# Modulation blocks of the two mixers on ScalarE and GpSimd instead of TensorE

## The chip, the cores and the metric

The kernel runs on one core of a Trainium2 chip. The time is that of one execution in device microseconds (us); of several runs the median counts. The engines are TensorE (PE in the profile, PEld for its weight loads), VectorE (DVE), ScalarE (ACT), GpSimd (POOL) and SyncE (SP), which issues the loads.

## The reference

Two layers of an encoder over 256 tokens of width 1024. In each layer a vector `c` of 1024 numbers gives six modulation vectors of 1024, which shift, scale and gate the layer's two parts: a mixer (a recurrence beside attention) and a feed-forward part, which is dense in layer 0 and a choice of 2 of 8 experts in layer 1.

```python
c_act = jax.nn.silu(c)
for l in range(DEPTH):
    mod = c_act @ ada_w[l] + ada_b[l]                 # 1024 x 6144 per layer
    shift1, scale1, gate1, shift2, scale2, gate2 = [m[:, None, :] for m in jnp.split(mod, 6, axis=-1)]
    h = rms_norm(x, norm1_g[l]) * (1 + scale1) + shift1
    ...                                               # input projection, recurrence, attention
    x = x + gate1 * ((g_lru * y_lru + g_mla * y_mla) @ w_out[l])
    h = rms_norm(x, norm2_g[l]) * (1 + scale2) + shift2
    ...                                               # feed-forward part f
    x = x + gate2 * f
```

The product `c_act @ ada_w[l]` is what the change is about. It is a row vector times a matrix of 24 MB per layer.

## The kernel before, in words

**Weights.** Every weight matrix is streamed once, in tiles of 1 MB (four times 128 rows by 512 columns of float32). SyncE issues the loads into a ring of four tiles, `raw0` to `raw3` (`load`, L148); a tile's slot is free again once its last reader is done. Where a matrix goes through TensorE in full precision, `split` (L176, L177) makes two halves of it: ACT casts the upper one (`wh`), DVE subtracts it for the lower one (`wl`), and each product is three matmuls (`mm3`, L309 to L311). So ACT and DVE work on every tile, and PE waits for both.

**Modulation.** The 6144 columns of a layer are cut into blocks of 512, called (layer, group, block); groups 0 to 5 are shift1, scale1, gate1, shift2, scale2, gate2. A block is two tiles of 1 MB, the halves of its 1024 rows. Most blocks are computed beside the dense part or ahead of the first mixer, by DVE (`ada`, L394, and others). Eight are computed inside the mixers by `ada_pe`: in mixer 0 the blocks 2_0, 2_1 (gate1), 4_0, 4_1 (scale2), 3_0, 3_1 (shift2) of layer 0; in mixer 1 the blocks 5_0, 5_1 (gate2) of layer 1. There PE multiplies each 128x512 piece by `c32`, a column of `c_act` widened to 32 columns, into a quarter of one PSUM tile (L363, eight matmuls per block). The tile is copied to `aacc` in SBUF: with the bias row added by DVE (L369) in the row blocks, groups 2 and 5, or by ACT (L371) in the column blocks, groups 3 and 4.

**What follows a block.** `ada_done` lets GpSimd sum `aacc` over the 128 partitions (`partition_all_reduce`, L318, a routine from a library). For a row block that is the end: the result is the gate row. For a column block GpSimd then keeps a diagonal (`affine_select`, L321), and `ada_cols` lets ACT sum it into columns (four activations, L341, the first ordered behind the cast that was last issued), to which DVE adds the bias (L348). `ada_cols` runs when a later block takes its accumulator, and once more at the mixer's end.

**The mixer.** `mixer` writes the work as a sequence of weight tiles: latents, `ck`, `q`, `kv`, then 16 tiles `t0` to `t15`, then the output projections. Its table `adas` says behind which tile a block stands. Eight attention heads (`head`, L976) and the steps of the recurrence hang on units of the same sequence. Attention normalizes q and k: GpSimd adds the epsilon and raises to the power -1/2 (`head_norm`, L938 and L939, into `rk` and `rq`); DVE scales the row maxima by `rq` (L997) and ACT the exponentials (L1000). GpSimd has little else to do.

**Order.** Each engine runs its own instructions in their order, and waits for others by semaphores. That order is made when the program is built, by a scheduler that goes by its own estimates of durations; `pr.order` adds a rule that one instruction stands behind another. So moving a block moves many instructions around it.

Of the kernel before, what the change touches and what calls it, by code (L numbers as in the profile page):

```python
# [14 lines left out]
AF = mybir.ActivationFunctionType  # L15
OP = mybir.AluOpType
# [4 lines left out]
D = 1024  # L21
# [200 lines left out]
def encoder(ctx: ExitStack, tc, x, c, positions, params, ada_w, ada_b, w_in, w_uq, w_ukv, w_o_mla,  # L222
            lru_gate_w, w_o_lru, w_out, ffn_w_gate, ffn_w_up, ffn_w_down, moe_router,
            moe_w_gate, moe_w_up, moe_w_down, out):
    nc = tc.nc
    V, A, G, T = nc.vector, nc.scalar, nc.gpsimd, nc.tensor
# [33 lines left out]
    cact = ct("cact", [P, KD])  # L260
    c32 = ct("c32", [P, KD, 32])
# [20 lines left out]
    brow = bt("brow", [P, 512])  # L282
# [5 lines left out]
    pr = Program(tc, list(cut_ring), dma_ahead=3, split_ahead=2)  # L288
# [11 lines left out]
    cur = {}  # L300
# [27 lines left out]
    def ada_acc(nm, more):  # L328
        n_acc[0] += 1
        if ada_q and ada_q[0][4] <= n_acc[0] - (ADA_KEEP if more else 1):  # L330
            ada_cols()
        tag, b = (("lraw0", 1), ("aacc", 2), ("lraw1", 1), ("aacc", 2))[n_acc[0] % 4] if more else ("aacc", 2)
        return wp.tile([P, 512], F32, tag=tag, name=f"aacc_{nm}", bufs=b)
# [16 lines left out]
            rn = (R_N1 if grp == 1 else R_N2) + 4 * blk  # L350
            V.scalar_tensor_tensor(dst, dst, 1.0, cols[l][:, rn:rn + 4], op0=OP.add, op1=OP.mult)

    def ada_pe(l, grp, blk, ring="a"):

        nm = f"{l}_{grp}_{blk}"
        box = {}

        def half(h, raw):
            if h == 0:
                box["ps"] = cur["ada_ps"](f"apa_{nm}")  # L360
            ps = box["ps"]
            for kk in range(4):
                T.matmul(ps[32 * kk:32 * kk + 32, :], c32[:, 4 * h + kk, :], raw[:, kk, :], start=h == 0, stop=h == 1)  # L363
            if h == 0:
                return
            acc = ada_acc(nm, False)
            if grp in (2, 5):
                nc.sync.dma_start(brow[0:1, :], ada_b[l:l + 1, grp * D + 512 * blk:grp * D + 512 * blk + 512])
                V.tensor_add(acc, ps, brow)  # L369
            else:  # L370
                A.copy(acc, ps)  # L371
            ada_done(l, grp, blk, acc)

        for h in range(2):
            W(ada_w[l], 4 * h, 4, grp * D + 512 * blk, 512, "raw", lambda raw, h=h: half(h, raw), ring)
# [223 lines left out]
    def mixer(l):  # L599
# [525 lines left out]
        def half_tiles(ap, c0, acc_fn, i):  # L1125
            W(ap, 4 * i, 4, c0, 512, "k", lambda q, h_, l_: acc_fn(4 * i + 2 * q, h_, l_))

        adas = {0: {"ck": (0, 2, 0), "q": (0, 2, 1), "t5": (0, 4, 0), "t7": (0, 4, 1), "t9": (0, 3, 0), "t11": (0, 3, 1)},
                1: {"t7": (1, 5, 0), "t9": (1, 5, 1)}}[l]

        def mark(name):
            if name in adas:
                ada_pe(*adas[name])

        def chunks(pos):
            for k in range(KD):
# [791 lines left out]
```

## Time and profile before

| | |
|---|---|
| median of 3 runs | 1452.67 us (1451.45 to 1455.13) |
| the profiled execution | 1453.3 us, span 1451.6 us |
| PE busy | 1390.5 us, 96% of the span |
| DVE busy | 1061.6 us, 73% |
| ACT busy | 840.8 us, 58% |
| GpSimd busy | 144.3 us, 10% |

The span is what the profiler saw from the first instruction to the last of one execution; the rest of the execution's time lies around it. A busy share is an average over the whole program; the work of the change stands in two stretches, mixer 0 (to about 263 us) and mixer 1 (about 560 to 660 us). Rows of a timeline give the start and the duration in us, and in brackets how long the engine sat idle before and what it waited for ("issue": for nothing that the profile shows).

### The profile page before, as it was taken

The numbers are of one execution on the slowest core, as the hardware profiler recorded it, in microseconds if no ns is written. First come the engines' busy times: TensorE is split into PE (matmuls) and PEld (weight loads), VectorE is DVE, ScalarE is ACT, GpSimd is POOL, SyncE is SP. The second block draws the span as 40 slices with busy tenths as digits, with TensorE's granted clock in tenths as the row PEclk, the third lists the DMA queues.
The fourth block names the chain that finished last, engine by engine and source line by source line (L and its number), as shares of the span: only waits on it lengthen the run. The fifth ranks groups of instructions, "written<-read, shape, count | busy, mean of one in ns | idle before, by whom it ended". The sixth has DMA issues, their size and how long they took to land.

```text
span 1451.6 us, 20969 instructions
## 1 busy us (share of the span) xinstructions
PE 1390.5 (96%) x7786; PEld 1058.7 (73%) x7786; DVE 1061.6 (73%) x1460; ACT 840.8 (58%) x1279; POOL 144.3 (10%) x116
## 2 busy tenths in 40 slices
PE   7999999899999899999999999999999999999997
PEld 5977667799988788677877744788784368888732
DVE  4799877799899499877599613898882069988711
ACT  3678854544544498854388513787781167877500
POOL 1021220033232002010021000000000000000000
PEclk8999999999999999999999999999999999999999
DMA  9784667989986254565778999999899999998996
GB/s 320 248 261 131 232 235 240 306 291 320 320 307 220 87 175 158 173 208 204 291 280 312 335 409 414 411 388 397 279 388 378 403 408 400 378 360 312 384 399 268
DMA packets 169134, 436.59 MB, mean 301 GB/s; under 512 B 7336, under 2 KB 63016, under 8 KB 157760
## 3 DMA queue, kind: packets, MB, share of 16 engines
q1 hardware_dynamic: 168400, 434.48, 81.8%
q8 instruction: 63, 1.03, 0.3%
q10 hardware_dynamic: 560, 0.66, 0.1%
q14 instruction: 47, 0.39, 0.1%
q0 software_dynamic: 64, 0.03, 0.0%
HBM read 434.10 MB, written 1.05 MB: 300 GB/s over the span
## 4 chain that ended last, share of the span: by engine, by line
PE 71%; DVE 16%; issue 5%; ACT 4%; DMA 2%; POOL 1%; SPq 0%; DVEq 0%; ACTq 0%; POOLq 0%
DVE wl L177 7%; PE eg L1752 4%; PE dn L310 4%; PE dn L1775 4%; PE dn L311 4%; PE eu L1752 4%; PE dn L309 4%; PE eg L310 3%; PE eg L311 3%; PE eg L309 3%; PE eu L310 3%; PE eu L309 3%; PE eu L311 3%; DVE aacc L394 2%; PE u L309 1%
## 5 line engine op out<-in xcount | busy, mean ns | idle before, releaser
L177 DVE TENSOR_TENSOR wl<-wr,wh 128x1024 fp32r<-128x1024 f32 (+2 forms) x556 | 638.9, 1182 | 86.2 <-ACT wh L176 83.1
L176 ACT CAST wh<-wr 128x1024 fp32r<-128x1024 f32 (+2 forms) x556 | 547.1, 1000 | 207.1 <-PE dn L311 31.7
L1673 DVE TENSOR_TENSOR act<-sg,eu 128x512 f32<-128x512 f32 (+2 forms) x42 | 25.1, 612 | 143.6 <-PE eu L1752 102.5
L310 PE MATMUL eg<-wl,xe 128*128 128x512 f32 x240 | 91.7, 382 | 4.2 <-DVE wl L177 2.9
L310 PE MATMUL eu<-wl,xe 128*128 128x512 f32 x240 | 90.4, 377 | 1.6 <-DVE wl L177 1.6
L311 PE MATMUL eu<-wh,xe 128*128 128x512 f32 x240 | 89.8, 374 | 0.0
L311 PE MATMUL eg<-wh,xe 128*128 128x512 f32 x240 | 89.7, 374 | 0.0
L310 PE MATMUL dn<-wl,ahl 128*128 128x512 f32 x220 | 87.5, 401 | 0.8 <-DVE wl L177 0.8
L311 PE MATMUL dn<-wh,ahl 128*128 128x512 f32 x220 | 85.8, 393 | 0.0
L309 PE MATMUL eg<-wh,xe 128*128 128x512 f32 x240 | 81.0, 379 | 0.0
L309 PE MATMUL eu<-wh,xe 128*128 128x512 f32 x240 | 80.4, 374 | 0.0
L394 DVE SCALAR_TENSOR_TENSOR aacc<-wr,cact,aacc 128x512 f32<-128x512 f32 x84 | 74.9, 895 | 1.1
L309 PE MATMUL dn<-wh,ahl 128*128 128x512 f32 x220 | 75.7, 397 | 0.0
L1752 PE MATMUL eu<-wr,xe 128*64 128x512 f32 (+1 forms) x288 | 66.0, 562 | 0.0
L1752 PE MATMUL eg<-wr,xe 128*64 128x512 f32 (+1 forms) x288 | 65.3, 564 | 0.0
L1664 ACT ACTIVATE sg<-eg 128x512 f32<-128x512 f32 (+2 forms) x42 | 20.6, 534 | 73.2 <-PE eg L1752 73.2
L318 POOL PARTITION_ALL_REDUCE aacc<-aacc x12 | 49.0, 4083 | 132.7 <-DVE aacc L394 67.9
L1775 PE MATMUL dn<-wr,aT 128*64 128x512 f32 x264 | 58.9, 596 | 0.0
L310 PEld LDWEIGHTS eg<-wl,xe 128*128 128x128 f32 x240 | 45.2, 188 | 16.0 <-DVE wl L177 7.2
L310 PE MATMUL g<-wl,hTh 128*128 128x512 f32 x128 | 51.8, 405 | 2.8 <-DVE wl L177 2.8
L310 PEld LDWEIGHTS eu<-wl,xe 128*128 128x128 f32 x240 | 45.1, 188 | 12.3 <-DVE wl L177 3.3
L309 PE MATMUL g<-wh,hTh 128*128 128x512 f32 x128 | 52.8, 418 | 0.0
(422 smaller groups left out, 3205.1 us busy)
## 6 DMA issues: line engine op xcount, KB each, us to landing
wr<-in_moe_w_down_dram SPq DMA_DIRECT2D x88, 1024.0 KB, 7.8
wr<-in_moe_w_gate_dram SPq DMA_DIRECT2D x64, 1024.0 KB, 9.4
wr<-in_moe_w_up_dram SPq DMA_DIRECT2D x64, 1024.0 KB, 7.7
wr<-in_ada_w_dram SPq DMA_DIRECT2D x48, 1024.0 KB, 7.7
wr<-in_w_in_dram SPq DMA_DIRECT2D x30, 1024.0 KB, 5.3
wr<-in_moe_w_gate_dram SPq DMA_DIRECT2D x32, 768.0 KB, 11.0
wr<-in_moe_w_up_dram SPq DMA_DIRECT2D x32, 768.0 KB, 5.7
wr<-in_ffn_w_gate_dram SPq DMA_DIRECT2D x13, 1024.0 KB, 8.0
```

Of the source, the lines that this page charges most:

```text
L176: i1 = self.nc.scalar.copy(hi, src)
L177: i2 = self.nc.vector.tensor_sub(lo, src, hi.bitcast(F32))
L309: T.matmul(o, lh, rh, start=start, stop=False)
L310: T.matmul(o, lh, rl, start=False, stop=False)
L311: T.matmul(o, ll, rh, start=False, stop=stop)
L318: G.partition_all_reduce(tot, acc, P, bass_isa.ReduceOp.add)
L394: V.scalar_tensor_tensor(acc, raw[:, kk, :], cact[:, k:k + 1], acc, op0=OP.mult, op1=OP.add)
L1664: A.activation(sg[r, cs_], p[r, cs_], AF.Silu)
L1673: V.tensor_mul(act[r, cs_], B["sg"][j][r, cs_], p[r, cs_])
L1752: T.matmul(ps[0][64 * j:64 * j + 64, :sl.stop - sl.start], B["xe", e][:, k, :], raw[:, sl], start=k == 0, stop=k == KD - 1)
L1775: T.matmul(B["dn"][0][64 * m:64 * m + 64, :], a_, raw[:, 512 * m:512 * m + 512], start=f == 0, stop=f == FC - 1)
```

## The change

The eight blocks are computed by `ada_mix` in place of `ada_pe`. Of the four 128x512 pieces of a tile, two are multiplied by their entry of `c_act` in place by ACT, two by GpSimd (both L363 in the changed file); GpSimd adds the pieces, and in row blocks the bias row, into `aacc` (L372, L374, L377). The PSUM tile and its copy are gone; `ada_done` and `ada_cols` are unchanged. The first of ACT's products of each half stands behind the cast that was last issued. Five of the six blocks of mixer 0 and one of mixer 1 stand behind another tile than before. In all 64 matmuls, four DVE adds and four ACT copies go, and 32 ACT products, 32 GpSimd products and 60 GpSimd additions come. Lines behind the new function lie 7 further down (L938 becomes L945, L997 becomes L1004, L1000 becomes L1007).

```diff
--- before.py
+++ after.py
@@ -350,26 +350,33 @@
             rn = (R_N1 if grp == 1 else R_N2) + 4 * blk
             V.scalar_tensor_tensor(dst, dst, 1.0, cols[l][:, rn:rn + 4], op0=OP.add, op1=OP.mult)
 
-    def ada_pe(l, grp, blk, ring="a"):
+    def ada_mix(l, grp, blk, ring="a"):
 
         nm = f"{l}_{grp}_{blk}"
+        rowk = grp in (2, 5)
         box = {}
 
         def half(h, raw):
+            for kk in range(4):
+                k = 4 * h + kk
+                if kk % 2:
+                    G.tensor_scalar(raw[:, kk, :], raw[:, kk, :], cact[:, k:k + 1], None, op0=OP.mult)
+                    continue
+                i1 = A.activation(raw[:, kk, :], raw[:, kk, :], AF.Copy, scale=cact[:, k:k + 1])
+                if kk == 0:
+                    pr.order(i1, pr.last[0])
             if h == 0:
-                box["ps"] = cur["ada_ps"](f"apa_{nm}")
-            ps = box["ps"]
-            for kk in range(4):
-                T.matmul(ps[32 * kk:32 * kk + 32, :], c32[:, 4 * h + kk, :], raw[:, kk, :], start=h == 0, stop=h == 1)
-            if h == 0:
-                return
-            acc = ada_acc(nm, False)
-            if grp in (2, 5):
-                nc.sync.dma_start(brow[0:1, :], ada_b[l:l + 1, grp * D + 512 * blk:grp * D + 512 * blk + 512])
-                V.tensor_add(acc, ps, brow)
-            else:
-                A.copy(acc, ps)
-            ada_done(l, grp, blk, acc)
+                acc = box["acc"] = ada_acc(nm, False)
+                if rowk:
+                    nc.sync.dma_start(brow[0:1, :], ada_b[l:l + 1, grp * D + 512 * blk:grp * D + 512 * blk + 512])
+                    G.tensor_tensor(acc, raw[:, 0, :], brow, op=OP.add)
+                else:
+                    G.tensor_tensor(acc, raw[:, 0, :], raw[:, 1, :], op=OP.add)
+            acc = box["acc"]
+            for kk in range(0 if h else 1 if rowk else 2, 4):
+                G.tensor_tensor(acc, acc, raw[:, kk, :], op=OP.add)
+            if h:
+                ada_done(l, grp, blk, acc)
 
         for h in range(2):
             W(ada_w[l], 4 * h, 4, grp * D + 512 * blk, 512, "raw", lambda raw, h=h: half(h, raw), ring)
@@ -1125,12 +1132,12 @@
         def half_tiles(ap, c0, acc_fn, i):
             W(ap, 4 * i, 4, c0, 512, "k", lambda q, h_, l_: acc_fn(4 * i + 2 * q, h_, l_))
 
-        adas = {0: {"ck": (0, 2, 0), "q": (0, 2, 1), "t5": (0, 4, 0), "t7": (0, 4, 1), "t9": (0, 3, 0), "t11": (0, 3, 1)},
-                1: {"t7": (1, 5, 0), "t9": (1, 5, 1)}}[l]
+        adas = {0: {"ck": (0, 2, 0), "t1": (0, 2, 1), "t4": (0, 4, 0), "t6": (0, 4, 1), "t8": (0, 3, 0), "t10": (0, 3, 1)},
+                1: {"t7": (1, 5, 0), "t10": (1, 5, 1)}}[l]
 
         def mark(name):
             if name in adas:
-                ada_pe(*adas[name])
+                ada_mix(*adas[name])
 
         def chunks(pos):
             for k in range(KD):
```

The scheduler's order of GpSimd's instructions shows a row that the source does not name: a bare `ISA`, ahead of a library routine that follows arithmetic and ahead of arithmetic that follows a library routine. In the trace of the kernel before it is called MODIFY_POOL_CONFIG. The first place is GpSimd's queue in mixer 0 from the end of block 2_0 to the normalizations of k and q (`vv`, `rk`, `rq`); before:

```order
L318 ISA gate_103<-aacc_2_0_861 128x512
L952 COPY k_869<-kr_645 128x8x32 x2
L318 ISA gate_103<-aacc_2_1_928 128x512
L938 ISA
L938 TENSOR_SCALAR vv_1190<-vv_1190 128x16
L939 TENSOR_TENSOR rk_1189<-vv_1190,mhalf 128x16
L938 TENSOR_SCALAR vv_1307<-vv_1307 128x16
L939 TENSOR_TENSOR rq_1306<-vv_1307,mhalf 128x16
```

After, from the normalization of k on (`wr` are the tiles of ada_w, `cact` is silu of c):

```order
L945 TENSOR_SCALAR vv_1179<-vv_1179 128x16
L372 TENSOR_TENSOR aacc_2_1_1257<-wr_1040,brow 128x512
L946 TENSOR_TENSOR rk_1178<-vv_1179,mhalf 128x16
L377 TENSOR_TENSOR aacc_2_1_1257<-aacc_2_1_1257,wr_1040 128x512 x3
L377 TENSOR_TENSOR aacc_2_1_1257<-aacc_2_1_1257,wr_1071 128x512 x4
L318 ISA
L318 ISA gate_103<-aacc_2_1_1257 128x512
L945 ISA
L945 TENSOR_SCALAR vv_1319<-vv_1319 128x16
L363 TENSOR_SCALAR wr_1276<-wr_1276,cact 128x512
L946 TENSOR_TENSOR rq_1318<-vv_1319,mhalf 128x16
```

The whole of block 2_1 and two bare ISA rows now stand between the two normalizations.

The second place is GpSimd's queue for the column blocks 4_1 and 3_0 of mixer 0; before:

```order
L318 ISA aacc_4_1_1883<-aacc_4_1_1883 128x512
L321 AFFINE_SELECT aacc_4_1_1883<-aacc_4_1_1883 128x512
L318 ISA aacc_3_0_2014<-aacc_3_0_2014 128x512
L321 AFFINE_SELECT aacc_3_0_2014<-aacc_3_0_2014 128x512
```

After, from the reduction of 4_1 to that of 3_0:

```order
L318 ISA aacc_4_1_1822<-aacc_4_1_1822 128x512
L374 ISA
L374 TENSOR_TENSOR aacc_3_0_1959<-wr_1774 128x512
L321 AFFINE_SELECT aacc_4_1_1822<-aacc_4_1_1822 128x512
L377 TENSOR_TENSOR aacc_3_0_1959<-aacc_3_0_1959,wr_1774 128x512
L363 TENSOR_SCALAR wr_1806<-wr_1806,cact 128x512
L377 TENSOR_TENSOR aacc_3_0_1959<-aacc_3_0_1959,wr_1774 128x512
L363 TENSOR_SCALAR wr_1806<-wr_1806,cact 128x512
L377 TENSOR_TENSOR aacc_3_0_1959<-aacc_3_0_1959,wr_1806 128x512 x4
L318 ISA
L318 ISA aacc_3_0_1959<-aacc_3_0_1959 128x512
```

Between two reductions there are now nine or more instructions of arithmetic and two bare ISA rows, where there was one selection. In all, the bare rows go from 3 to 11 in mixer 0 and from 1 to 3 in mixer 1.

The third place is ACT's queue around its reading of block 3_1, the last of mixer 0 (L341); before, up to the second head behind it:

```order
L371 COPY aacc_3_1_2171<-apa_3_1_0_2153 128x512
L341 ACTIVATE aacc_3_1_2171,ada_100<-aacc_3_1_2171 128x128 x3
L176 CAST wh_2195<-wr_2111 128x1024
...
L1000 ACTIVATE pr_0_2264,sm_0_2261<-s_0_2257,mx_0_2260,rq_1306 128x256 x2
...
L341 ACTIVATE aacc_3_1_2171,ada_100<-aacc_3_1_2171 128x128
L1000 ACTIVATE pr_0_2349,sm_0_2346<-s_0_2342,mx_0_2345,rq_1306 128x256 x2
```

After:

```order
L1007 ACTIVATE pr_0_2296,sm_0_2293<-s_0_2289,mx_0_2292,rq_1318 128x256 x2
...
L1007 ACTIVATE pr_0_2381,sm_0_2378<-s_0_2374,mx_0_2377,rq_1318 128x256 x2
L176 CAST wh_2245<-wr_2132 128x1024
L176 CAST wh_2261<-wr_2132 128x1024
L341 ACTIVATE aacc_3_1_2147,ada_100<-aacc_3_1_2147 128x128 x3
L176 CAST wh_2313<-wr_2165 128x1024
L176 CAST wh_2331<-wr_2165 128x1024
```

The last two heads (L1007) stand ahead of the reading of block 3_1 where they stood behind it, and the casts of the output projections follow it.

## Rows read from the trace of the kernel before

**Rows 1.** The page, parts 1 and 4: busy time by engine; the chain by engine.
```profile
PE 1390.5 (96%) x7786; PEld 1058.7 (73%) x7786; DVE 1061.6 (73%) x1460; ACT 840.8 (58%) x1279; POOL 144.3 (10%) x116
...
PE 71%; DVE 16%; issue 5%; ACT 4%; DMA 2%; POOL 1%; SPq 0%; DVEq 0%; ACTq 0%; POOLq 0%
```

**Rows 2.** Windows: stretch, length, busy us (instructions) of PE, PEld, DVE, ACT, POOL; clock, DMA.
```profile
60.00:140.00 80.00, 73.91 (x492) 62.52 (x491) 74.63 (x134) 64.55 (x117) 17.22 (x10) 1.00 0.65 211
140.00:220.00 80.00, 76.72 (x381) 54.41 (x382) 62.32 (x106) 55.37 (x121) 19.03 (x8) 0.98 0.65 224
560.00:640.00 80.00, 75.11 (x399) 56.90 (x400) 74.77 (x135) 60.22 (x103) 11.53 (x4) 1.00 0.53 178
```

**Rows 3.** Windows, L363 alone: stretch, length, busy us of PE and PEld.
```profile
60.00:260.00 200.00, 13.62 (x96) 2.75 (x96) 0.99 0.67 224
560.00:660.00 100.00, 3.85 (x32) 0.84 (x32) 1.00 0.52 174
```

**Rows 4.** Groups of POOL's instructions by form: busy us, mean ns; idle before.
```profile
L318 POOL PARTITION_ALL_REDUCE aacc<-aacc x12 | 49.0, 4083 | 132.7 <-DVE aacc L394 67.9 <-ACT aacc L371 64.8
L318 POOL PARTITION_ALL_REDUCE gate<-aacc x8 | 30.3, 3787 | 128.4 <-DVE aacc L394 61.9 <-DVE aacc L369 59.6 <-issue 6.9
L321 POOL TENSOR_SCALAR_AFFINE_SELECT aacc<-aacc 128x512 f32<-128x512 f32 x12 | 13.8, 1148 | 0.9
L1538 POOL TENSOR_TENSOR xr<-xr,xn 128x512 f32<-128x512 f32 x4 | 6.8, 1691 | 34.5 <-ACT xn L1533 34.5
...
L1540 POOL TENSOR_TENSOR xn<-xr,xn 128x512 bf16<-128x512 f32 x4 | 5.6, 1388 | 12.3 <-ACT xn L1536 12.3
```

**Rows 5.** Timeline of POOL in mixer 0: start us, duration us, instruction, idle before.
```profile
71.51 1.25 POOL L908 TENSOR_TENSOR rs<-ssq,mhalf 128x4 f32<-128x4 f32 x1
79.67 3.25 POOL L318 PARTITION_ALL_REDUCE gate<-aacc  x1 [6.90 <-issue]
...
107.26 1.09 POOL L938 TENSOR_SCALAR vv<-vv 128x16 f32<-128x16 f32 x1 [15.90 <-DVE vv L937]
...
122.29 3.20 POOL L939 TENSOR_TENSOR rq<-vv,mhalf 128x16 f32<-128x16 f32 x1
155.53 3.25 POOL L318 PARTITION_ALL_REDUCE aacc<-aacc  x1 [30.05 <-ACT aacc L371]
...
205.62 3.31 POOL L318 PARTITION_ALL_REDUCE aacc<-aacc  x1 [14.57 <-ACT aacc L371]
209.01 0.63 POOL L321 TENSOR_SCALAR_AFFINE_SELECT aacc<-aacc 128x512 f32<-128x512 f32 x1
```

**Rows 6.** Timeline around 75 us, DVE.
```profile
75.33 0.69 DVE L369 TENSOR_TENSOR aacc<-apa,brow 128x512 f32<-128x512 f32 x1
```

**Rows 7.** Groups of ACT's instructions by form.
```profile
L176 ACT CAST wh<-wr 128x512 fp32r<-128x512 f32 x16 | 10.0, 623 | 0.4 <-PE y L310 0.4
```

**Rows 8.** Timeline in the expert part, 747 to 756 us, DVE and POOL.
```profile
747.09 1.22 DVE L177 TENSOR_TENSOR wl<-wr,wh 128x1024 fp32r<-128x1024 f32 x1
747.15 2.18 POOL L1538 TENSOR_TENSOR xr<-xr,xn 128x512 f32<-128x512 f32 x1 [2.06 <-ACT xn L1533]
...
748.33 2.08 DVE L177 TENSOR_TENSOR wl<-wr,wh 128x1024 fp32r<-128x1024 f32 x1
...
755.23 1.17 POOL L1540 TENSOR_TENSOR xn<-xr,xn 128x512 bf16<-128x512 f32 x1 [5.90 <-ACT xn L1536]
```

**Rows 9.** Line L318: durations in ns (least, median, most), first and last start.
```profile
L318 POOLq MODIFY_POOL_CONFIG  x8: 6/8/11, 72.7 to 570.4; - x8
```

**Rows 10.** Timeline from 470 to 481 us, the end of the dense part, ACT and POOL.
```profile
472.44 0.19 ACT L427 ACTIVATION_READ_ACCUMULATOR fax<-xs 128x1 f32 x1
...
479.75 0.30 POOL L451 TENSOR_SCALAR nrv<-ss 128x1 f32<-128x1 f32 x1 [7.52 <-issue]
```

**Rows 11.** DMA issues from 100 to 210 us: count, size, median us to landing.
```profile
wr<-in_ada_w_dram SPq DMA_DIRECT2D x8, 1024.0 KB, 5.3
```

**Rows 12.** Timeline around 136 us, DVE.
```profile
135.86 0.16 DVE L997 TENSOR_TENSOR mx<-mx,rq 128x2 f32<-128x2 f32 x1
```

**Rows 13.** Timeline of ACT from 200 to 263 us.
```profile
209.68 0.31 ACT L341 ACTIVATE aacc<-aacc 128x128 f32<-128x128 f32 x1 [4.15 <-POOL aacc L321]
...
262.70 1.06 ACT L176 CAST wh<-wr 128x1024 fp32r<-128x1024 f32 x1 [1.62 <-PE wo L311]
```

## The prediction

> **What bounds the kernel now.** I read the page's first and fourth parts first: TensorE (PE) is busy 96% of the span and makes 71% of the chain that ended last, while GpSimd (POOL) is busy 10%, 116 instructions in all [rows 1]. That says where the weight of the whole lies, not what the two mixers can bear. So the next view was the busy time of each engine in the stretches where the blocks stand: mixer 0 from 60 to 220 us and mixer 1 from 560 to 640 us [rows 2]. PE has 74 to 77 of each 80 us, and VectorE (DVE) nearly as much: 5.4, 17.7 and 5.2 us idle in the three. ScalarE (ACT) has 15 to 25 us idle, and GpSimd 61 to 68. What is removed from PE comes from the same view of L363 alone [rows 3]: 13.62 us in mixer 0 and 3.85 us in mixer 1, 17.5 in all. GpSimd's own rows, by group and one by one, then price what is added [rows 4, 5].
>
> **The change part by part.**
>
> *Removed.* 17.5 us of PE, of which the share on the chain would be a gain if everything else stayed covered. Also four DVE adds at 0.69 [rows 6], 2.7 us, and four ACT copies of the same size.
>
> *Products on ACT.* 32 copies with a scale, priced by the cast of a 128x512 tile at 0.623 [rows 7]: 15 us in mixer 0 against 40 idle [rows 2]. I cost them at nothing themselves; their place matters below.
>
> *GpSimd's arithmetic.* A row block has 4 products and 8 additions on GpSimd, a column block 4 and 7. For an addition the rows give a mean of 1.691 and 1.388 and single ones of 1.17 and 2.18 [rows 4, 8]; I take 1.4, near the cheaper group since the dear one has more contention in it, with ends of 1.17 and 2.18. A product reads one tensor; the nearest row is the affine selection over 128x512, 0.63 at its shortest and 1.148 in the mean [rows 4, 5]: 0.8, ends 0.63 and 1.15.
>
> *GpSimd's library switch.* This is the term that the diff does not show. In the order, a bare ISA row stands wherever GpSimd goes from tensor arithmetic to the partition reduction, or back; in the trace the same thing is a MODIFY_POOL_CONFIG [rows 9]. Its price: after the power at 71.51 (1.25 us) GpSimd has nothing to run until the reduction at 79.67, 6.90 us of "issue", though that reduction's input came from DVE at 75.33 + 0.69 = 76.0 [rows 5, 6]. On the way back, the mean square was read out at 472.44 + 0.19 = 472.6, and the first arithmetic row starts at 479.75, behind 7.52 us of "issue" [rows 10]. So about 7.2 us in either direction. Before, almost every switch lies in a pause: the reductions at 155.53 to 205.62 stand 13 to 21 us apart with no arithmetic between them [rows 5]. After, mixer 0 has 11 such rows instead of 3, and mixer 1 has 3 instead of 1.
>
> The Trainium skill, GPSIMD Engine Reference, section 2.1, says that the first call after new code is loaded pays some 6 us, measured 5.95. This trace has 6.90 and 7.52, and the measurement decides; by the page's figure the nine switches below would cost 11 us less.
>
> *The chain on GpSimd in mixer 0.* Per column block: 4 x 0.8 + 7 x 1.4 + reduction 4.1 + selection 1.15 + two switches 14.4 = 32.6 us, against 13 to 21 between reductions before. So GpSimd sets the pace. I sum it from the normalization of k, whose input comes at 107.26 [rows 5], later by 2.7 because DVE has been held back by the first block: 110. Behind it on GpSimd, in the changed order, stand 36 additions (50.4), 16 products (12.8), 9 switches (64.8), 5 reductions at 4 (20), 4 selections (4.6), and the two normalizations at 0.8 + 3.2 (8.0): 160.6 us. To this come waits, which I put at 13.8: 5 for ACT's products of block 2_1, queued behind activations of the recurrence, and 8.8 for tiles whose slot comes free late and whose 1 MB takes 5.3 us to land [rows 11]. End of block 3_1: 110 + 160.6 + 13.8 = 284.4, where before it was 209.01 + 0.63 = 209.7.
>
> Two things hang on this chain. The power for q, ready at 125.5 before [rows 5], comes behind block 2_1 and both its switches: 110 + 4 + 11.2 + 5 + 7.2 + 4 + 7.2 + 0.8 + 0.8 + 3.2 = 153. Its first reader on DVE stood at 135.86 [rows 12], so DVE waits some 15 us there with the lower halves of the weights queued behind it, and PE with DVE. And ACT's reading of block 3_1, which waited 4.15 us before [rows 13], has the mixer's remaining casts queued behind it. Before, 262.7 - 209.7 = 53.0 us passed from there to the mixer's last cast [rows 13]; in the changed order two heads stand ahead of it, and I take 11 us off that rest. Mixer 0: 284.4 - 209.7 - 11 = +64.
>
> The ends: with 1.17 and 0.63 and no waits the chain ends at 259.6, +39; with 2.18 and 1.15 at 318, +98.
>
> *Mixer 1.* Two row blocks put 28.8 us of arithmetic, 8 of reductions and 21.6 of switches on GpSimd, where 11.53 of 80 us are used [rows 2]. It just fits. What remains is a tile or two loaded late, since a block holds its two slots until its last addition, and DVE's losses (next paragraph): +5, between -3.85 (all hidden, PE's share gone) and +16 (DVE's whole loss, no idle time used).
>
> *The port.* With GpSimd adding from 747.15 to 749.33, DVE's subtraction at 748.33 took 2.08 us, where the one before took 1.22 [rows 8]. So an addition on GpSimd takes about 0.8 from DVE; a product, with half the operands, I estimate at 0.4. In mixer 0 that is 44 x 0.8 + 24 x 0.4 = 45 us against 23 idle. In the forecast these losses lie mostly inside the stretches in which DVE waits for GpSimd, so they aren't added.
>
> The Trainium skill, SBUF — State Buffer, "SBUF: two separate sides", calls the shared ports an exclusive lock: the engine that comes second waits for the whole instruction. The trace agrees, 2.08 beside 1.22 [rows 8]; by that rule alone, without switches, the time is that of rival A.
>
> *Sum.* +64 + 5 = +69 on the profiled execution's 1453.3 us: 1522.3. The median of the runs lies 0.6 under that execution, so 1521.
>
> **Rivals.**
>
> A, the port alone: the switches overlap other work, and only DVE's losses tell. Mixer 0: 45 - 23 idle - 2.7 for the removed adds = 19; mixer 1: 16 - 5.2 idle = 11. 1483. For it: DVE is 93% busy in two of the stretches [rows 2]. Against it: 6.90 and 7.52 us in which GpSimd ran nothing [rows 5, 10], and additions that leave it no pause.
>
> B, PE's gain: GpSimd's long chain is covered, because nobody needs the modulation before the mixer's end, and PE's 17.5 us count with its 71% of the chain: -12.4, 1440. For it: 61 to 68 us idle on GpSimd in each stretch [rows 2]. Against it: the powers for k and q are in GpSimd's queue, and ACT waited on block 3_1 already before [rows 13]. It decides once a column block costs less than its spacing, 13 to 21 us; I work out 32.6.
>
> C, one direction of the switch costs nothing, because the arithmetic never leaves memory: 4 switches fewer on the chain, 284.4 - 28.8, so +35 + 5: 1493. Against it: 7.52 on the way back [rows 10].
>
> D, every GpSimd operation at its contended price: 1453.3 + 98 + 11 = 1562. For it: DVE leaves few pauses in which GpSimd can take the port. Against it: DVE itself stalls as soon as GpSimd sets the pace, and that frees the port.
>
> **How the numbers follow.** The forecast 0.66, A 0.14, C 0.08, D 0.06, B 0.06. A measurement of this kernel tells a change from none from about 0.3%, 4.4 us. Faster is B, 0.06. The same is the edge of A in which DVE's pauses take all of the losses, 0.03. Slower is the rest, 0.91. The range takes in A and C, and the forecast's ends (1453.3 + 39 - 3.85 - 0.6 = 1488 below, 1453.3 + 98 + 16 - 0.6 = 1567 above) except its dearest part: 1470 to 1550. Left out are B, D, the edge of A and some 0.04 of the forecast's own top, 0.19 together.
>
> **What would show it.** Right: gaps of about 7 us marked "issue" before the reductions and before the first arithmetic after them; ACT's reading of block 3_1 (L341) idle for tens of us on GpSimd's L321; DVE idle for some 15 us on the power for q; GpSimd busy far beyond 144 us, and PE idle between 200 and 300 us. The port: the mean of L177 above 1182 ns. Wrong: a reduction that starts as soon as its additions end, or a mixer 0 whose last cast still stands near 263 us. If L177 grows but no engine waits long on GpSimd, it was A; if PE's idle time in mixer 0 shrinks, B.

## The result and the profile after

The changed kernel takes 1550.38 us in the median (1549.09 to 1551.35, 4 runs) against 1453.08 us before: a ratio of 1.067 (95% interval 1.0655 to 1.0682). It is slower, as forecast, by 97 us where 69 were forecast; the median lies just above the top of the range.

The page of the kernel after, parts 1 and 4, to be held against [rows 1]:

```profile
PE 1405.4 (91%) x7658; PEld 1076.6 (69%) x7658; DVE 1095.5 (71%) x1456; ACT 859.3 (55%) x1307; POOL 292.7 (19%) x208
...
PE 57%; DVE 16%; issue 9%; POOL 9%; DMA 4%; ACT 4%; SPq 1%; DVEq 0%; POOLq 0%; ACTq 0%
```

GpSimd is still busy only 19% of the span. It has 9% of the last chain, though, where it had 1%. "Issue", the kind of wait under which the library switches show, went from 5% to 9%, and PE's share fell from 71% to 57%.

Where the time went is read from three marks that both kernels pass: GpSimd's first row of the norm behind mixer 0 (L451 before, L458 after), the same behind the dense part, and the reduction of the router's bias at mixer 1's end. In the kernel after:

```profile
346.18 0.62 POOL L458 TENSOR_SCALAR nrv<-ss 128x1 f32<-128x1 f32 x1 [12.31 <-ACT ax L434]
...
560.01 0.31 POOL L458 TENSOR_SCALAR nrv<-ss 128x1 f32<-128x1 f32 x1 [7.08 <-issue]
...
773.84 1.31 POOL L1068 PARTITION_ALL_REDUCE rbias<-rbias  x1
```

Before, the second stood at 479.75 [rows 10], the first and the third here:

```profile
269.20 0.62 POOL L451 TENSOR_SCALAR nrv<-ss 128x1 f32<-128x1 f32 x1 [11.80 <-ACT ax L427]
...
676.05 1.37 POOL L1061 PARTITION_ALL_REDUCE rbias<-rbias  x1
```

So mixer 0 lost 77.0 us, the dense part 3.3 and mixer 1 17.5; from there to the end both kernels take 775.6 to 775.9 us.

The stretches of mixer 0 after, in the columns of [rows 2]:

```profile
60.00:140.00 80.00, 62.02 (x371) 58.02 (x370) 74.76 (x105) 56.74 (x104) 50.27 (x30) 0.81 0.55 175
140.00:220.00 80.00, 57.03 (x255) 41.97 (x254) 52.85 (x84) 49.21 (x93) 46.25 (x29) 0.87 0.32 107
220.00:300.00 80.00, 51.53 (x181) 37.24 (x181) 42.72 (x63) 28.46 (x61) 41.41 (x26) 0.76 0.46 155
```

No engine is near full after 140 us. That is how a chain of waits looks: PE falls to 51.5 of 80 us and the loads to 107 GB/s, where they had 224. The mean of the granted clock, 1.00 and 0.98 before [rows 2], is 0.76 to 0.87, so for a part of these stretches TensorE ran at the lower of its two levels. GpSimd has much of that chain. Its timeline for the last column block (3_1), with the switches on both sides:

```profile
261.34 3.25 POOL L318 PARTITION_ALL_REDUCE aacc<-aacc  x1 [8.02 <-issue]
271.76 1.57 POOL L363 TENSOR_SCALAR wr<-wr,cact 128x512 f32<-128x512 f32 x1 [7.17 <-issue]
273.31 0.64 POOL L321 TENSOR_SCALAR_AFFINE_SELECT aacc<-aacc 128x512 f32<-128x512 f32 x1
273.95 1.55 POOL L363 TENSOR_SCALAR wr<-wr,cact 128x512 f32<-128x512 f32 x1
275.48 1.25 POOL L374 TENSOR_TENSOR aacc<-wr 128x512 f32<-128x512 f32 x1
276.73 1.55 POOL L363 TENSOR_SCALAR wr<-wr,cact 128x512 f32<-128x512 f32 x1
278.26 1.25 POOL L377 TENSOR_TENSOR aacc<-aacc,wr 128x512 f32<-128x512 f32 x1
279.50 1.60 POOL L363 TENSOR_SCALAR wr<-wr,cact 128x512 f32<-128x512 f32 x1
281.06 6.62 POOL L377 TENSOR_TENSOR aacc<-aacc,wr 128x512 f32<-128x512 f32 x5
295.57 3.74 POOL L318 PARTITION_ALL_REDUCE aacc<-aacc  x1 [7.88 <-issue]
```

From one reduction to the next pass 34.2 us without another wait: two switches of 7.17 and 7.88, and arithmetic end to end between them. Before, the spacing was 13 to 21 us [rows 5]. One thing was not forecast: a product (L363) takes 1.55 to 1.60 us even where an addition takes 1.25.

### The profile page after: what moved, and what is told of

Its sections match the earlier page's. It is cut to its first block, busy times and chain, and to the rows that moved or that the text cites. A ratio compares the mean times of both kernels' runs of the same rounds, so it can differ in the third digit from the quotient of the medians.

```text
span 1549.7 us, 20872 instructions
## 1 busy us (share of the span) xinstructions
PE 1405.4 (91%) x7658; PEld 1076.6 (69%) x7658; DVE 1095.5 (71%) x1456; ACT 859.3 (55%) x1307; POOL 292.7 (19%) x208
## 4 chain that ended last, share of the span: by engine, by line
PE 57%; DVE 16%; issue 9%; POOL 9%; DMA 4%; ACT 4%; SPq 1%; DVEq 0%; POOLq 0%; ACTq 0%
DVE wl L177 7%; PE eg L1759 4%; PE dn L1782 4%; PE eu L1759 4%; PE dn L310 3%; PE dn L311 3%; PE dn L309 3%; POOL aacc L377 3%; DVE aacc L401 3%; PE eg L310 3%; PE eg L311 3%; PE eg L309 3%; POOL wr L363 3%; PE eu L310 2%; PE eu L309 2%
## 5 line engine op out<-in xcount | busy, mean ns | idle before, releaser
L177 DVE TENSOR_TENSOR wl<-wr,wh 128x1024 fp32r<-128x1024 f32 (+2 forms) x556 | 649.9, 1204 | 116.0 <-ACT wh L176 112.7
L363 POOL TENSOR_SCALAR wr<-wr,cact 128x512 f32<-128x512 f32 x32 | 68.2, 2134 | 94.7 <-DMA wr<-in_ada_w_dram 51.1
L377 POOL TENSOR_TENSOR aacc<-aacc,wr 128x512 f32<-128x512 f32 x52 | 76.0, 1461 | 3.0
L310 PE MATMUL g<-wl,hTh 128*128 128x512 f32 x128 | 56.5, 441 | 18.5 <-DVE wl L177 18.4
L318 POOL PARTITION_ALL_REDUCE aacc<-aacc x12 | 44.7, 3721 | 99.1 <-DVE aacc L401 66.6
```

Source lines behind the costliest of these rows:

```text
L177: i2 = self.nc.vector.tensor_sub(lo, src, hi.bitcast(F32))
L310: T.matmul(o, lh, rl, start=False, stop=False)
L318: G.partition_all_reduce(tot, acc, P, bass_isa.ReduceOp.add)
L363: G.tensor_scalar(raw[:, kk, :], raw[:, kk, :], cact[:, k:k + 1], None, op0=OP.mult)
L377: G.tensor_tensor(acc, acc, raw[:, kk, :], op=OP.add)
```

## The experiments

Marks as above; "m0" is what mixer 0 lost against the profiled execution before (269.2 us), "m1" the length of mixer 1 (196.3 before).

| kernel | median us | m0 | m1 |
|---|---|---|---|
| changed | 1550.4 | +77.0 | 213.8 |
| TensorE sums over the partitions | 1528.5 | +54.4 | 221.0 |
| GpSimd on 8 of 512 columns | 1494.0 | +31.6 | 200.8 |
| all products on ACT | 1534.4 | +70.0 | 207.3 |
| places of before | 1574.8 | +94.5 | 218.7 |
| TensorE's sum one block later | 1510.1 | +43.9 | 211.7 |
| before, with GpSimd copies | 1496.8 | +30.1 | 207.0 |
| without ACT's rule | 1555.2 | +79.3 | 215.3 |
| before, with TensorE's sum | 1460.9 | +6.8 | 202.1 |
| late sum, tiles released early | 1501.6 | +38.8 | 212.3 |
| late sum, 8 of 512 columns | 1458.2 | -1.4 | 205.2 |
| products in other forms | 1550.0 | +75.3 | 213.8 |
| before, at the new places | 1465.5 | +20.2 | 195.3 |
| two more switches per block | 1631.4 | +148.3 | 226.7 |
| mixer 0 only | 1539.4 | +78.9 | 196.4 |

The kernel before ran at 1453.2 to 1454.8 beside them (medians). Where the profiled execution is not the median, m0 and the median differ by some us (the profiled one took 1474.3 us for "before, at the new places" and 1639.1 for "two more switches").

In five kernels TensorE sums in both mixers: runs 1, 5, 8, 9 and 10 below. There the last mark, itself a library routine, is the first one behind arithmetic, and it stands behind a gap of its own of 5.8 to 6.0 us. From that mark to the end these kernels take 769.7 to 770.3 us, where the others take 775.6 to 777.6. So their m1 is to be read some 6 us shorter: mixer 1 of run 1, for one, is about as long as that of the change, and that of run 8 as long as before.

**1. No library routine in the mixers.**

```diff
-                ada_done(l, grp, blk, acc)
+                ada_red(l, grp, blk, acc)
```

The cut shows the call alone. `ada_red` multiplies the accumulator by ones on TensorE; ACT copies the result for gate rows, and DVE adds the bias for columns.

> The changed kernel, but TensorE sums the accumulators of the mixers' eight blocks over the partitions (a product with ones, and a copy by ACT for gate rows), so GpSimd runs no library routine in the mixers and switches no library; its 92 products and additions stay. Theory (GpSimd's chain with its switches paces the mixers): a column block costs GpSimd 7 x 1.44 + 4 x 1.70 = 17 us instead of some 36, about the spacing of the tiles, so most of the 97 us goes: 1455 to 1490. Rival A (the port alone, DVE's losses beside GpSimd's arithmetic): the arithmetic is unchanged, so the time stays near 1530 to 1550. Rival P (the new places of the blocks and the new order of the engines): stays near 1550 too.

Measured 1528.5 (1.0508, 1.049 to 1.0525): 22 us less than the change, and a miss for the theory as put (1455 to 1490); it lies just under what A and P wanted (1530 to 1550). The waits in mixer 0 of this kernel (who waited for whom: us in all, times, longest) say why:

```profile
PE ared L361 <- POOL aacc L395: 18.6, 4, 8.4
PEld ared L357 <- POOL aacc L395: 13.8, 2, 9.0
PE ared L357 <- POOL aacc L395: 13.2, 2, 8.8
```

TensorE's sum stands in TensorE's queue, and the matmuls behind it wait until GpSimd has done its last addition. The experiment took one wait away and brought another, so by itself it does not price the switches.

**2. Switches without arithmetic.**

```diff
-G.tensor_tensor(acc, acc, raw[:, kk, :], op=OP.add)
+G.tensor_tensor(acc[:, :8], acc[:, :8], raw[:, kk, :8], op=OP.add)
```

One line of the edit; the products and the first additions are cut alike, and DVE clears the accumulator first. What the other 504 columns hold is left out.

> The changed kernel, but GpSimd multiplies and adds only 8 of each 512 columns; the rest of the accumulator is zero, so the modulation is wrong in 504 of 512 columns of these blocks. Number and order of GpSimd's instructions, the switches and the reductions stay. Theory: the chain in mixer 0 loses some 79 - 52 x 0.2 = 69 us of arithmetic and keeps 9 switches of 7.8 and 5 reductions: it ends near 231 instead of 300 and still behind before's 209.7; with what the rest wins back the time is 1460 to 1485. Rival A: without arithmetic nothing is left of the loss, 1450 to 1456. Rival P: near 1550.

Measured 1494.0 (1.0275, 1.0258 to 1.0292): 39 us are lost with hardly any arithmetic, 9 us above the theory's range. The waits on nothing but a switch before GpSimd's reductions (L318) and products (L363), in mixer 0 of this kernel:

```profile
POOL aacc L318 <- issue: 37.2, 4, 10.2
POOL wr L363 <- issue: 30.7, 4, 8.8
...
POOL gate L318 <- issue: 17.3, 2, 10.0
```

That is 85 us of gaps in ten switches. A and P, as put, are out: the port alone would leave nothing, the order alone all of it.

**3. Products on ACT.**

```diff
-                if kk % 2:
-                    G.tensor_scalar(raw[:, kk, :], raw[:, kk, :], cact[:, k:k + 1], None, op0=OP.mult)
-                    continue
```

> The changed kernel, but ACT makes all eight products of a block; GpSimd only adds. Theory: 16 products at 1.70 us leave GpSimd's chain of mixer 0 (27 us), while ACT gains 16 x 0.72 = 12 us there, and mixer 1 wins part of its 23 us of products: 1505 to 1530. Rival A: a product takes about 0.4 us from DVE, 32 of them 13 us: 1537. Rival P: near 1550.

Measured 1534.4 (1.0558, 1.0537 to 1.058), 4 us above the theory's range. Of the 27 us of products on the chain of mixer 0, 7 came back there: GpSimd now waits for ACT's products, 10.6 us at L371, and single additions run longer (mean 1.58 on the chain against 1.44). The chain ends at 284.4, 15.6 us earlier than in the changed kernel, and the mixer still ends only 7 earlier, so the chain is not all that paces it. Mixer 1 gave back 6.5. A's number fits better (1537); this run does not tell them apart.

**4. The places of before.**

```diff
-{"ck": (0, 2, 0), "t1": (0, 2, 1), "t4": (0, 4, 0), "t6": (0, 4, 1), "t8": (0, 3, 0), "t10": (0, 3, 1)}
+{"ck": (0, 2, 0), "q": (0, 2, 1), "t5": (0, 4, 0), "t7": (0, 4, 1), "t9": (0, 3, 0), "t11": (0, 3, 1)}
```

> The changed kernel with its blocks at the places of the kernel before (behind q, t5, t7, t9, t11 in mixer 0, and t7, t9 in mixer 1). Theory: GpSimd's chain is as long wherever its blocks start, and a later start only moves its end back: 1545 to 1575. Rival P (the new places are what costs): 1460 to 1500. Rival A: near 1550.

Measured 1574.8 (1.0831, 1.0813 to 1.0849), at the upper end of the theory. A later start moves the chain's end back, and ACT waits for it at L341, in mixer 0 of this kernel

```profile
ACT aacc L341 <- POOL aacc L321: 39.2, 4, 15.2
```

and in that of the changed kernel

```profile
ACT aacc L341 <- POOL aacc L321: 21.9, 3, 10.7
```

The new places are not what makes the change slower; at the old ones it costs 24 us more.

**5. TensorE's sum one block later.**

```diff
-                ada_red(l, grp, blk, acc)
+                red_q.append((l, grp, blk, acc))
```

The queue is emptied at the next block's second half, and at the mixer's end.

> As the kernel without library routines in the mixers (1528 us), but TensorE's sum over the partitions of a block is written one block later, so that TensorE's queue does not stand waiting for GpSimd's last addition (it waited 32 us for these in mixer 0). Theory B (that wait took the place of the switches): 1485 to 1510, and what is left is the time that GpSimd's arithmetic holds the tiles' slots and ACT's products. Rival A (the port alone makes up the rest): the wait was only a sign of work that is late anyway, so 1520 to 1530.

Measured 1510.1 (1.0387, 1.037 to 1.0405), the theory's upper end: TensorE's waits on GpSimd are gone (0.5 us is left in mixer 0), and 18 us with them. Without switches and without that wait, 56 us remain.

**6. GpSimd copies on the kernel before.**

```diff
+            for kk in range(6):
+                G.tensor_copy(raw[:, kk % 4, :], raw[:, kk % 4, :])
```

> The kernel before, TensorE's products and all, with 96 GpSimd copies of 128x512 added: six on each of the mixers' 16 modulation tiles, in place, after TensorE has read them. Nobody reads their result; the tile's slot is held until they are done; a copy needs no library switch. Theory (waiting on GpSimd's results and held slots, not the port): 12 copies at some 0.7 us hold a pair of slots 8 us longer, 1453 to 1470. Rival A (the port): 96 x 0.4 to 0.8 = 38 to 77 us of DVE against 28 us idle, 1463 to 1503, with the mean of L177 in the mixers well above 1.25 us.

Measured 1496.8 (1.0303, 1.0286 to 1.0321), in A's range. But the kernel isn't the clean case that I took it for: reductions stand behind the copies in GpSimd's queue, and ACT waited 25.8 us for them at L341, beside what DVE lost (from 60 to 260 us L177 took 1.35 us over 128x1024 in the mean, where it took 1.22 before). It shows that more GpSimd work costs time even where nobody reads it, not by which way.

**7. Without the rule on ACT's products.**

```diff
-                if kk == 0:
-                    pr.order(i1, pr.last[0])
```

> The changed kernel without the rule that puts ACT's first product of each half behind the cast that was last issued. Theory (GpSimd's chain with its switches): GpSimd waited for ACT's products only in places (17.2 us in mixer 1, a few in mixer 0), and a part of that comes back: 1530 to 1552. Rival O (the rule is what couples GpSimd to the casts, and so to the slots, and makes most of mixer 1's loss): 1510 to 1530.

Measured 1555.2 (1.069, 1.0671 to 1.0709), 3 us above the theory's range and 5 above the change: the rule costs nothing. Rival O is out.

**8. TensorE's sum on the kernel before.** The same `ada_red`, behind `ada_pe`.

> The kernel before with TensorE's sum over the partitions for the mixers' eight blocks in place of GpSimd's reduction and selection and ACT's reading; products on TensorE as before. It asks whether GpSimd's part was worth anything on the chain before. Theory: before, reductions and switches lay in pauses, except for ACT's wait of 4.15 us and VectorE's losses of about 2 us at each reduction: 1440 to 1453. Rival W (TensorE's queue waits for the copy of the accumulator each time, 8 times 1 to 2 us): 1453 to 1465.

Measured 1460.9 (1.005, 1.0034 to 1.0067), 7 us slower than before: taking the reductions and switches off GpSimd won nothing on balance, which fits with their lying in pauses but does not prove it, since TensorE's sums came in their place. By the marks the 7 us lie in mixer 0. Rival W gave the number, but its wait is not in the trace (ACT waited 1.3 us and DVE 3.7 us for these sums); which wait made the 7 us stays open.

**9. Tiles released early.** To run 5, two of the lines that change:

```diff
-                    G.tensor_scalar(raw[:, kk, :], raw[:, kk, :], cact[:, k:k + 1], None, op0=OP.mult)
+                G.tensor_scalar(box["acc"], xs[:, 0, :512], raw[:, kk, 0:1], None, op0=OP.mult)
...
-                G.tensor_tensor(acc, acc, raw[:, kk, :], op=OP.add)
+                G.tensor_tensor(acc, acc, xs[:, 0, :512], op=OP.add)
```

The modulation of these blocks is left out.

> As the kernel with TensorE's late sum (1510 us, no switches in the mixers), but GpSimd's operands of 128x512 are columns of the resident x in place of the modulation tiles; of a tile it reads only one column, as the factor of its product. So GpSimd does as many operations of the same size, but a tile's slot comes free after its two products instead of after the additions behind them (the modulation of these blocks is left out). Theory S (held slots are what is left of the loss: two of four slots are gone for 30 us and more, and the weights wait): 1465 to 1490. Rival A (the port: DVE's losses beside GpSimd's arithmetic): unchanged, 1500 to 1512.

Measured 1501.6 (1.0326, 1.0309 to 1.0343): 8.5 us of the 56 came back with the slots; the rest stays, as rival A said. The 8.5 may be too low a price for the slots: in this kernel TensorE's sums of mixer 0 wait again, 6.3 us for GpSimd and 5.8 for ACT. In the changed kernel itself, with its switches, no run prices them.

**10. Late sum, hardly any arithmetic.** Run 5 with run 2's edit.

> As the kernel with TensorE's late sum, but GpSimd multiplies and adds only 8 of each 512 columns (the rest of the modulation of these blocks is left out). Neither switches nor long arithmetic are left, so what remains is the new order, ACT's products and the new places. Theory: the switches with the reductions (39 us in the kernel with small arithmetic) and the arithmetic (56 us in the kernel with the late sum) make up the 97 us between them: 1450 to 1465. Rival P (a part of the loss lies in the order and in ACT's products): 1470 or more.

Measured 1458.2 (1.0031, 1.002 to 1.0042), as the theory said. With neither switches nor arithmetic, 5 us remain for order, places, ACT's products and TensorE's sums together. Held against it, run 9 shows what GpSimd's arithmetic does to DVE. DVE in mixer 0 of run 9 (55 to 308 us) and of run 10 (55 to 268 us), first the stretch in the columns of [rows 2], then one group of DVE, a form that both run 24 times:

```profile
55.00:308.00 253.00, 210.62 (x1062) 171.80 (x1061) 205.87 (x297) 156.59 (x269) 128.15 (x80) 0.91 0.58 192
```
```profile
L838 DVE SCALAR_TENSOR_TENSOR uc<-uT,cols,uc 128x256 f32<-128x256 f32 x24 | 19.1, 840 | 0.5 <-ACT uc L835 0.5
```

and run 10:

```profile
55.00:268.00 213.00, 198.74 (x1074) 163.66 (x1073) 169.51 (x305) 157.15 (x271) 58.25 (x79) 0.98 0.68 227
```
```profile
L835 DVE SCALAR_TENSOR_TENSOR uc<-uT,cols,uc 128x256 f32<-128x256 f32 x24 | 10.4, 481 | 1.2 <-ACT uc L832 1.2
```

Nearly the same DVE work is busy for 205.9 us beside GpSimd's arithmetic and for 169.5 without it, 36 us more, in a mixer that is 40 us longer. DVE stands idle about as long in both, 47 and 43 us: its idle time took up next to nothing of what it lost. That these losses set the mixer's length is argued from the two sums and not shown by a run of its own, for PE too was busy 12 us longer, at a mean granted clock of 0.91 instead of 0.98, and TensorE's sums waited as said under run 9.

**11. Forms of the product.**

```diff
+                    if kk == 1:
+                        G.tensor_tensor(raw[:, kk, :], raw[:, kk, :], cact[:, k:k + 1].to_broadcast([P, 512]), op=OP.mult)
+                    else:
+                        G.tensor_scalar(raw[:, kk, :], raw[:, kk, :], 0.5, None, op0=OP.mult)
```

> The changed kernel, but GpSimd's products come in two other forms: one of a half as a multiplication of two tensors, with the factor broadcast along the row, the other by a constant 0.5 in the instruction (wrong values in these pieces). It asks what made the product cost 1.56 us at its shortest, above the two-operand addition's 1.25. Theory (the factor read from a tile per partition costs it): the product of two tensors takes 1.25, the constant 0.65 to 1.25; the chain loses 5 to 10 us in mixer 0 and the time is 1535 to 1548. Rival (a float product is slow on GpSimd in any form): both 1.5 or more and the time stays at 1550.

GpSimd's timeline of this kernel at the last block:

```profile
271.23 1.03 POOL L364 TENSOR_TENSOR wr<-wr,cact 128x512 f32<-128x512 f32 x1 [6.78 <-issue]
272.23 0.63 POOL L321 TENSOR_SCALAR_AFFINE_SELECT aacc<-aacc 128x512 f32<-128x512 f32 x1
272.86 1.53 POOL L366 TENSOR_SCALAR wr<-wr 128x512 f32<-128x512 f32 x1
274.38 1.25 POOL L377 TENSOR_TENSOR aacc<-wr 128x512 f32<-128x512 f32 x1
```

On the forms both guesses were wrong; on the time the rival's held. A product of two tensors, the factor broadcast, takes 1.03, less than an addition; the product by a constant takes 1.53, as long as by a column. Of these forms the instruction with a scalar is the slow one. The time did not move (1550.0): half of the products got 0.5 us cheaper, some 4 us of the chain in mixer 0, and the mark there moved by 1.7.

**12. The kernel before at the new places.** Run 4's edit the other way, with TensorE's products.

> The kernel before, with its blocks at the places of the changed kernel (behind t1, t4, t6, t8, t10 in mixer 0, t7 and t10 in mixer 1). It asks whether the places alone cost or win anything while TensorE makes the products. Theory: GpSimd's part is hidden at either places, except for ACT's wait of 4.15 us on the last block, which an earlier start takes away: 1446 to 1456. Rival P: a share of the change's loss lies in the places, 1465 or more.

Measured 1465.5 (1.007, 1.0052 to 1.0087), 12 us slower: a miss for the theory, at the lower end of what rival P wanted. ACT waits longer for GpSimd at the new places, 19.2 us at L341 instead of 4.15 (in the profiled execution, the slowest of the five). So places and engines go together: the new ones cost 12 us with TensorE and win 24 with GpSimd (run 4).

**13. Two more switches per block.**

```diff
+                G.partition_all_reduce(tny, acc[:, 0:1], P, bass_isa.ReduceOp.add)
+                G.tensor_tensor(acc[:, 0:1], acc[:, 0:1], ones[:, 0:1], op=OP.mult)
                 ada_done(l, grp, blk, acc)
```

> The changed kernel with one more library call and one more arithmetic operation for each of the eight blocks, both of one column (a reduction of one column, then a multiplication by one): two more library switches for each block, 12 in mixer 0 and 4 in mixer 1, and hardly any more work. Theory (the switches stand in line on GpSimd's chain, which paces mixer 0): 12 x 7.7 us and 6 x 2 us of small operations = 104 us, less pauses of some 10 us in which GpSimd waited anyway, so +90 to +105 there, and +10 to +35 in mixer 1: 1650 to 1690. Rival A (the port makes the loss, and a switch mostly overlaps): under 1600.

Measured 1631.4 (1.1222, 1.1203 to 1.1241), 81 us more than the change. In the profiled execution it is 88, of which 71 in mixer 0 and 13 in mixer 1: 5.9 for each of 12 switches in mixer 0, with the small operations in it. The theory wanted 90 to 105 there, A under 50 in all; the time lies between the two ranges, nearer to the theory's. GpSimd's timeline of it around the reduction of block 3_0:

```profile
312.51 0.40 POOL L380 PARTITION_ALL_REDUCE tny<-aacc  x1 [9.78 <-issue]
319.74 1.57 POOL L364 TENSOR_SCALAR wr<-wr,cact 128x512 f32<-128x512 f32 x1 [6.83 <-issue]
321.30 0.18 POOL L381 TENSOR_TENSOR aacc<-aacc,ones 128x1 f32<-128x1 f32 x1
321.47 1.55 POOL L364 TENSOR_SCALAR wr<-wr,cact 128x512 f32<-128x512 f32 x1
328.96 3.25 POOL L319 PARTITION_ALL_REDUCE aacc<-aacc  x1 [5.94 <-issue]
339.09 1.25 POOL L375 TENSOR_TENSOR aacc<-wr 128x512 f32<-128x512 f32 x1 [6.88 <-issue]
```

Each change of library is its own gap, whether 512 columns follow or one. The gaps in mixer 0 of this kernel last 7.5 us in the mean, twelve of them 90, so nearly four fifths of that comes out in the mixer's length.

**14. Mixer 0 only.** Mixer 1's two blocks by `ada_pe`, at their old places.

> The change in mixer 0 alone: the two blocks of mixer 1 are computed by TensorE at their old places. Theory (the two mixers add up, as the stretches of the trace say: 77 and 17.5 us): 1550.4 - 17.5 = 1533, at most 2 us more or less. Rival (the late start after mixer 0 also shifts mixer 1, so that part of its loss stays): 1538 to 1550.

Measured 1539.4 (1.0597, 1.0579 to 1.0614), 11 us less than the change and not 17.5, so by the times the rival's range. By the marks mixer 1 is back at 196.4 us, and it is mixer 0 that took 1.9 and the dense part 1.0 us more; the runs here lie between 1536.8 and 1541.2, and the profiled one is the fastest. That mixer 1's loss comes from its own blocks is shown; that the two add up, only to some us.

## Why the prediction was wrong

The direction, the mechanism and its place held; the size was 29 us short, 13 of it in mixer 0, 12.5 in mixer 1 and 3.3 in the dense part. Two terms of the sum were too small: the price of a product on GpSimd, and what mixer 1 loses. Held step by step against the trace after:

- **The chain on GpSimd paces mixer 0.** Right in the main, though run 3 shows that it is not all that does. It was to end at 284.4 and ended at 299.38 + 0.65 = 300.0, 15.6 late. From the normalization of k (113.9, forecast 110) its parts are: 36 additions 51.8 us (50.4), 5 reductions 17.1 (20), 4 selections 2.6 (4.6), both normalizations 7.4 (8.0), switches and waits together 80.1 (78.6), and 16 products 27.2 (12.8). **The step that failed is the price of a product on GpSimd**: "the nearest row is the affine selection ... 0.8, ends 0.63 and 1.15". It is 1.70 on the chain, 1.55 at its least, above the upper end; that is 14.4 of the 15.6 us. The groups on the chain, 113.8 to 300.1 us:

```profile
L377 POOL TENSOR_TENSOR aacc<-aacc,wr 128x512 f32<-128x512 f32 x31 | 44.8, 1444 | 1.6
L363 POOL TENSOR_SCALAR wr<-wr,cact 128x512 f32<-128x512 f32 x16 | 27.2, 1703 | 23.2 <-issue 14.2 <-DMA wr<-in_ada_w_dram 8.8
```

That one operand is cheaper than two was an argument, not a row; the rows held no GpSimd product of that size. What the missing price is worth in the time, run 3 bounds: without any product on GpSimd 16 us come back, 7 of them in mixer 0, and not the whole of what they last, since ACT's products are late next. So the wrong price accounts for the chain's late end; of the 13 us that mixer 0 lost beyond the forecast it accounts, as far as run 3 shows, for a part only, and what made the rest stays open.

- **What hangs on the chain.** DVE's wait for the power of q was 4.71 us, not 15: the power came at 155.78 (forecast 153), but DVE itself was late by then. ACT's wait for block 3_1, which was to be tens of us, was 5.31, but it is the last of three waits at L341, 21.9 us in all (shown under run 4). A third door, which the prediction had only as waits of the chain itself, is as wide: slots. In mixer 0 of the kernel after:

```profile
ACT wr L365 <- DMA wr<-in_ada_w_dram: 15.1, 3, 7.0
...
ACT wh L176 <- DMA wr<-in_w_in_dram: 9.5, 2, 8.1
...
DVE mx L1004 <- POOL rq L946: 4.7, 1, 4.7
```

ACT stood for tiles that had not landed, 15.1 us before its products and 9.5 before casts of `w_in`, while the loads ran at 107 GB/s. What kept the loads from starting is in SyncE's own waits in mixer 0, after and before:

```profile
SPq L148 <- POOL aacc L377: 124.9, 11, 24.0
```
```profile
SPq L148 <- PE apa L363: 30.4, 10, 8.2
```

By the profile SyncE waited 124.9 us to issue loads because GpSimd's additions were not yet done with a slot; TensorE's products had kept it 30.4. The rest behind the chain, 339.68 - 300.03 = 39.7, was right (42):

```profile
300.06 0.31 ACT L341 ACTIVATE aacc<-aacc 128x128 f32<-128x128 f32 x1 [5.31 <-POOL aacc L321]
...
339.68 1.06 ACT L176 CAST wh<-wr 128x1024 fp32r<-128x1024 f32 x1 [1.62 <-PE wo L311]
```

- **Mixer 1, the second step that failed.** Forecast +5 with an upper end of +16, measured +17.5. I had written that the arithmetic "just fits". It doesn't: block 5_1's products stand behind block 5_0's reduction and both its switches (8.31 + 3.69 + 6.99 us), its two tiles wait there, and four loads of the recurrence's output weights wait for slots, from SyncE and then from ACT:

```profile
704.60 39.59 SPq L148 DMA_DIRECT2D wr<-in_w_o_lru_dram  x4
```
```profile
743.06 1.99 ACT L176 CAST wh<-wr 128x1024 fp32r<-128x1024 f32 x2 [14.90 <-DMA wr<-in_w_o_lru_dram]
```

- **The dense part** was counted at nothing and cost 3.3 us; why stays open.

- **The switch** was right in size: 7.07 to 8.84 us in the chain's rows after, against 7.2. Its marginal worth is 5.9 (run 13).

- **The range.** The sum's own ends reached 1567 above (+98 there should be +97), and the range was cut at 1550 by leaving out the forecast's dearest part. The time came out in the part that was left out.

- **Rival A**, the port. It is real, and was priced too low: 30 us with DVE's idle time set against it, where runs 9 and 10 differ by 43, with DVE's own busy time in mixer 0 36 longer. In the changed kernel DVE's busy time in mixer 0 is as high (207.6 us from 55 to 346, 176.3 from 55 to 269 before), but there it lies beside GpSimd's chain. That would explain why taking the switches away did not give back 70 us: DVE's losses are next in line. The Trainium skill, SBUF — State Buffer, "SBUF: two separate sides", has the engine that comes second wait for the other's whole instruction. The 128x256 form that went from 481 to 840 ns in the mean agrees: the median of its 24 in run 9 is 484 ns, and the longest took 1522, 1.04 us more, which is within one GpSimd addition of 1.25. Arithmetic alone cost 56 us (run 5), switches alone 39 (run 2), both 97, neither 5 (run 10).

- **Rival B** (PE's gain) and **C** (one direction of the switch free) fell. Both directions cost some 7 us or more. PE's 13.6 us are not even gone from its busy time in mixer 0, in the columns of [rows 2], before and after:

```profile
55.00:269.00 214.00, 203.72 (x1134) 159.46 (x1132) 176.32 (x303) 148.64 (x281) 38.05 (x22) 0.99 0.68 227
```
```profile
55.00:346.00 291.00, 219.22 (x1042) 176.74 (x1040) 207.61 (x303) 161.78 (x301) 142.97 (x90) 0.85 0.51 169
```

Without the products PE was busy for 190.1 us before; after, the same matmuls take 219.2, at a mean granted clock of 0.85 instead of 0.99. Whether any of these 29 us lies on the path, no run here separates.

- **Rival D**, 1562, had additions at 2.18 and products at 1.15; additions were 1.44 and products 1.70, so its number lay near for the wrong reason.

No version of these beats the kernel before.

## What to carry to other kernels

An engine that is 10% busy can still be the wrong place for work: count its queue from the first input to the last reader, with every change of library in it, and compare that with the spacing at which the work arrives. Price each added form from a row of that very form, and where there is none, let the upper end of the range exceed the dearest operation of that engine and size. When an experiment takes a suspected cost away, read its trace for what came in its place before drawing a conclusion: here a queue that waited, then what DVE lost beside GpSimd.

## What the runs showed of the hardware

- A change between arithmetic and a library routine on GpSimd costs 6 to 10 us each way as read from the gaps (6.99 to 8.84 in the changed kernel's mixers), also for one column; added on the chain, it lengthened the mixer by 5.9 (run 13).
- On GpSimd, over 128x512 in float32, at their shortest in microseconds: selection 0.63, product of two tensors (one broadcast along the row) 1.03, sum of two 1.25, product with a scalar 1.48 by a constant and 1.55 by a column.
- Beside GpSimd's arithmetic single DVE operations lose about a microsecond while the median keeps its time. From run 10 to run 9 the median of the 128x256 form above went from 482 to 484 ns and the longest from 486 to 1522; of the subtraction L177 (all its forms in mixer 0) from 1218 to 1219 and from 1243 to 2219. In the mean the small ones lose more in proportion: 481 to 840 against 1219 to 1291 over 128x1024.
- Products taken off TensorE need not shorten its busy time: in mixer 0 after, where PE sat idle for 72 of 291 us (10 of 214 before), the mean granted clock was 0.85 instead of 0.99, and the matmuls that stayed were busy 29 us longer.
